# Attention stage with the transposes of the probabilities one unit behind the scores, a written-out order on four engines, and the gate row on ScalarE and GpSimd

## The chip, the cores and the metric

The kernel runs on one core of a Trainium2 chip. The time is device microseconds (us) of one run; three runs of the kernel before were timed, and their median counts. Five engines work side by side: TensorE (PE in the profile; PEld is its weight load), VectorE (DVE, `V` in the code), ScalarE (ACT, `S`), GpSimd (POOL, `G`) and SyncE (SP, `SY`), which here issues the loads and stores.

## The reference

One layer of a hybrid backbone, for one sequence of 512 latent tokens and 256 context tokens of width 2048: a common input projection, eight heads of a gated DeltaNet, eight heads of grouped-query attention (two key heads), gates on both, and one output projection. Everything is fp32. What bears on the change:

```python
mod = silu(c) @ w_ada + b_ada
shift, scale, gate = split(mod, 3)              # 2048 columns each
h = rms_norm(x, norm_w) * (1 + scale) + shift
qkv_g, z_g, gates, q_a, k_a, v_a, z_a = split_proj(h @ w_in)
...
s = einsum(q_blk, k_all) * HEAD_DIM ** -0.5     # 512 queries x 768 keys a head
p = softmax(s)
attn = einsum(p, v_all)
...
gdn_lat  = rms_norm(o_gdn, gdn_norm_w) * silu(z_g)
attn_lat = attn * silu(z_a)
y = concatenate([gdn_lat, attn_lat]) @ w_out
x = x + gate * y
return rms_norm(x, final_norm_w)
```

## The kernel before, in words

An fp32 product is made as three products of a high and a low half (`mm3`, lines 138 to 140): high x high, high x low, low x high. A weight piece of 128x512 is loaded by SP into `wraw`, ACT casts it to the high half `whi` (line 121), and POOL, or DVE where the caller says so, subtracts for the low half `wlo` (line 122). Each of the three has three buffers.

The program runs in stages. First come the modulation and the first projections, then the DeltaNet scans with further projections between them, up to about 924 us. Then comes the attention stage, which the change rewrites, to 1237.6 us, and then the output projection.

In the attention stage a head's 512 queries are taken as two units of 256 (`qp` 0 and 1, each with two blocks `qi` of 128). For a unit:

- `attn_scores`: PE makes the scores `s` (256 queries x 768 keys, one PSUM tile); DVE takes the maximum of each block (`mx`) and scales it, ACT makes exp and its sum (`pr`), DVE takes the reciprocal and scales `pr`.
- `attn_pt`: PE transposes `pr` in three groups of four blocks (tiles `pt`), ACT casts each to `pth`, DVE subtracts for `ptl`.
- `attn_values`: PE makes the output `o` from `pth`, `ptl` and the values, and DVE multiplies it into `M`, the input of the output projection.

`attn_norm` and `attn_qt` prepare the queries of the next head: `qtp` are transposes of the stored queries `qc` on PE; `qn` gets their norm (`hss`) and the rotary table, of which one product, `rt2`, is made on POOL; `qtp2` transposes back, and the halves are `qTh` and `qTl`.

PE would idle during the softmax, so the products of the gate path stand between: 16 tiles `zl`, each from 4 weight pieces, each piece 4 steps of 3 products. `fill(n)` puts n such steps at the place of the call; `FP`, `FS`, `FE`, `FV`, `FQ`, `FR` are the counts. After a tile, `z_steps` applies SiLU (ACT tanh, DVE `ze`) and multiplies into `M`. After every second head `gate_row` makes 512 columns of `gate`: 16 loads `graw` of `w_ada`, scaled and added up on DVE in `gacc` (line 1165), then summed over the partitions by a product with ones (`gater`) and stored.

After the stage, `M` is split into `mh` (ACT) and `ml` (DVE), and for each of four column blocks c the pieces of `w_out` (`wo`) are loaded and multiplied; `epilogue` applies gate, residual and final norm (`tt`, `yx`). For c below 3 the low half of an even piece k is made on POOL and of an odd one on DVE.

The order of PE's instructions is the order of the code throughout (`manual_schedule`); that of the other engines is set by the framework's scheduler. An engine runs its list in order.

## Time and profile before

| what | value |
|---|---|
| median of three runs | 1444.21 us (1441.69, 1444.21, 1445.38) |
| the profiled execution | 1441.82 us, span 1440.0 us, mean granted PE clock 0.976 |
| PE busy in the span | 1287.2 us (89%), 9406 instructions |
| PE weight load | 1027.4 us (71%) |
| DVE / ACT / POOL busy | 756.9 (53%) / 569.9 (40%) / 476.9 us (33%) |
| attention stage, 924.0 to 1237.6 us: PE / DVE / ACT / POOL busy | 288.77 / 189.98 / 123.63 / 100.58 of 313.60 us |

An engine's busy time is the sum of its recorded operations in the stretch. A group of instructions is shown by line, engine, operation and tiles (out<-in), with its count, busy time, mean and the idle time just before its members and what ended it. The granted clock is the share of full speed that the throttle gave PE.

### The profile page before, as it was taken

What the parts mean: (1) busy time and instruction counts of PE and PEld (TensorE: products, weight loads), DVE (VectorE), ACT (ScalarE), POOL (GpSimd) and SP (SyncE); (2) the same over time, 40 slices, a digit from 0 to 9 for tenths busy, and PEclk for the clock granted to TensorE, in tenths of its full rate; (3) what the DMA queues carried; (4) which work ended last, traced back from release to release, by engine and by line L of the source; (5) the groups of instructions that cost most, each with busy time, mean ns of one, the idle gap of its engine ahead of it and who ended that gap; (6) DMA issues with size and microseconds to landing.
All of it is one profiled execution on the core that took longest, in us unless ns stands there. A gap on an engine that the chain in (4) does not pass through costs nothing. (4 is left out here: it accounts for less than half of the span.)

```text
span 1440.0 us, 24845 instructions
## 1 busy us (share of the span) xinstructions
PE 1287.2 (89%) x9406; PEld 1027.4 (71%) x9406; DVE 756.9 (53%) x1680; ACT 569.9 (40%) x1441; POOL 476.9 (33%) x441
## 2 busy tenths in 40 slices
PE   3788888999998989898998988989898999998997
PEld 1455677888777777777777866777776777676785
DVE  3344694533756667665766243265747565433222
ACT  4111343343545454545444444334444433433221
POOL 1011212343343343434343444433333332233530
PEclk9999999999999999999999999999999999999999
DMA  9999522323222222131223432652525343464302
GB/s 307 264 287 283 152 67 62 66 71 81 55 68 48 61 57 60 44 74 50 61 56 69 119 105 70 189 170 69 163 71 153 81 126 95 155 228 137 93 28 107
DMA packets 263323, 161.95 MB, mean 112 GB/s; under 512 B 62946, under 2 KB 236091, under 8 KB 262179
## 3 DMA queue, kind: packets, MB, share of 16 engines
q1 hardware_dynamic: 263203, 160.36, 40.5%
q8 instruction: 74, 1.21, 0.3%
q14 instruction: 46, 0.38, 0.1%
HBM read 147.54 MB, written 12.77 MB: 111 GB/s over the span
## 5 line engine op out<-in xcount | busy, mean ns | idle before, releaser
L122 POOL TENSOR_TENSOR wlo_z<-wraw_z,whi_z 128x512 fp32r<-128x512 f32 x64 | 85.8, 1340 | 198.4 <-ACT whi_z L121 198.4
L156 PE MATMUL zl<-hhL,whi_z 128*128 128x512 f32 x256 | 108.6, 424 | 0.0
L156 PE MATMUL zl<-hlL,whi_z 128*128 128x512 f32 x256 | 103.4, 404 | 0.0
L214 POOL TENSOR_TENSOR sdh<-sth,egl 128x256 f32<-128x256 f32 x80 | 55.6, 695 | 142.6 <-DVE sth L756 68.3
L156 PE MATMUL zl<-hhL,wlo_z 128*128 128x512 f32 x256 | 102.5, 401 | 0.0
L735 ACT ACTIVATE oqh<-ksh,egsw 64x128 f32<-64x128 f32 x128 | 46.4, 362 | 118.9 <-DVE rh L730 118.1
L730 DVE SCALAR_TENSOR_TENSOR rh<-ksh,negeg,vtokh 64x128 f32<-64x128 f32 x176 | 61.3, 348 | 52.4 <-PE ksh L718 41.1
L139 PE MATMUL po<-wlo_wo,mh 128*128 128x512 f32 x192 | 77.0, 401 | 8.8 <-POOL wlo_wo L122 5.9
L138 PE MATMUL po<-whi_wo,mh 128*128 128x512 f32 x192 | 76.1, 399 | 1.7 <-ACT whi_wo L121 1.0
L140 PE MATMUL po<-whi_wo,ml 128*128 128x512 f32 x192 | 76.0, 396 | 0.0
L756 DVE TENSOR_TENSOR sth<-sdh,tsh 128x256 f32<-128x256 f32 x80 | 33.7, 421 | 76.8 <-PE tsh L750 56.4
L1165 DVE SCALAR_TENSOR_TENSOR gacc<-graw,scol,gacc 128x512 f32<-128x512 f32 x60 | 52.9, 882 | 22.4 <-DMA graw<-in_w_ada 21.8
L750 PE MATMUL tsh<-vsh,ktok 128*128 128x128 f32 x352 | 59.1, 291 | 5.7 <-ACT vnh L746 5.7
L122 POOL TENSOR_TENSOR wlo_wo<-wraw_wo,whi_wo 128x512 fp32r<-128x512 f32 x24 | 34.7, 1449 | 85.7 <-ACT whi_wo L121 85.7
L121 ACT CAST whi_z<-wraw_z 128x512 fp32r<-128x512 f32 x64 | 39.5, 618 | 53.8 <-PE zl L156 43.9
L750 PEld LDWEIGHTS tsh<-vsh,ktok 128*128 128x128 f32 x352 | 47.8, 195 | 17.6 <-ACT vnh L746 14.4
L122 POOL TENSOR_TENSOR wlo_qa<-wraw_qa,whi_qa 128x512 fp32r<-128x512 f32 x32 | 41.7, 1303 | 51.8 <-ACT whi_qa L121 42.8
L743 ACT ACTIVATE vsh<-tsh,cch 128x128 f32<-128x128 f32 x88 | 32.3, 367 | 64.5 <-PE tsh L739 61.6
L156 PEld LDWEIGHTS zl<-hhL,wlo_z 128*128 128x128 f32 x256 | 49.2, 192 | 12.0
L122 DVE TENSOR_TENSOR wlo_wo<-wraw_wo,whi_wo 128x512 fp32r<-128x512 f32 x24 | 19.9, 831 | 71.0 <-ACT whi_wo L121 68.5
L156 PEld LDWEIGHTS zl<-hhL,whi_z 128*128 128x128 f32 x256 | 49.4, 193 | 9.4 <-issue 0.8
L1109 PE MATMUL pt<-cmain,pr 128*128 128x128 f32 x192 | 33.4, 289 | 24.8 <-DVE pr L1098 18.3
(394 smaller groups left out, 3992.9 us busy)
## 6 DMA issues: line engine op xcount, KB each, us to landing
wada<-in_w_ada SPq DMA_DIRECT2D x128, 256.0 KB, 5.2
wraw_z<-in_w_in SPq DMA_DIRECT2D x64, 256.0 KB, 2.8
graw<-in_w_ada SPq DMA_DIRECT2D x64, 256.0 KB, 3.0
wraw_wo<-in_w_out SPq DMA_DIRECT2D x48, 256.0 KB, 2.9
wraw_qa<-in_w_in SPq DMA_DIRECT2D x32, 256.0 KB, 2.9
wraw_q<-in_w_in SPq DMA_DIRECT2D x28, 256.0 KB, 2.9
wraw_k<-in_w_in SPq DMA_DIRECT2D x28, 256.0 KB, 2.9
wraw_v<-in_w_in SPq DMA_DIRECT2D x28, 256.0 KB, 2.8
```

The costliest lines, as they stand in the source:

```text
L121: S.copy(hi, raw)
L122: (lo_eng or G).tensor_tensor(out=lo, in0=raw, in1=hi, op=ALU.subtract)
L138: T.matmul(out, lhsT=lh, rhs=rh, start=start, stop=False, skip_group_check=True)
L139: T.matmul(out, lhsT=lh, rhs=rl, start=False, stop=False, skip_group_check=True)
L140: T.matmul(out, lhsT=ll, rhs=rh, start=False, stop=stop, skip_group_check=True)
L156: T.matmul(pl, lhsT=lw, rhs=rt[0][:, k], start=st, stop=sp, skip_group_check=True)
L214: eng.tensor_tensor(out=out, in0=x, in1=y, op=ALU.mult)
L730: V.scalar_tensor_tensor(out=r[rows], in0=ks[rows, d], scalar=gsc["negeg"][rows, gcol:gcol + 1], in1=vtok[rows, p], op0=ALU.mult, op1=ALU.add)
L735: S.activation(oq[rows, v, p - 2], ks[rows, d], AF.Copy, scale=gsc["egsw"][rows, gcol:gcol + 1])
L750: T.matmul(ts[:, d], lhsT=ktok[:, p, half], rhs=vs, start=True, stop=True, skip_group_check=True)
L756: V.tensor_tensor(out=sn, in0=sd, in1=ts[:, 0:2], op=ALU.add)
L1165: V.scalar_tensor_tensor(out=acc, in0=raw, scalar=scol[:, k:k + 1], in1=acc, op0=ALU.mult, op1=ALU.add)
```

## The change

1. The loop over heads becomes a loop over 17 units `u`. In a turn PE makes the scores of unit u, and the transposes and values of unit u-1 (`before`). The counts of gate steps become `FS`, `FP`, `FQ`, `FR` = 3, 3, 1, 3; the first unit gets 8 more.
2. In the attention loop the order of ACT, DVE and POOL is also that of the code.
3. `attn_scores` makes both maxima and then both exponentials; reciprocal and scaling move to `attn_over`, which stands behind the first and second group of transposes. `attn_norm` is a generator in three parts, spread over the odd unit of a head; the queries are first copied to SBUF by ACT, and `qn` has one buffer.
4. `fillers` asks for a weight piece two pieces ahead. The end of a tile (`z_over`) comes in the second step of the next tile.
5. The gate row is made over the whole stage, about one addition per weight piece: ACT scales `graw` in place (into `gacc` for the first of a column block), and POOL adds it to `gacc`. `graw` has 3 buffers, `gacc` 2.
6. In the output projection, the low half is made on DVE for every k of c below 3.
7. The transposes of a group run over the query block outside and the key block inside.

The number of PE's products and of loads and stores is the same. The core of the diff, without the removed lines of functions that are printed above:

```diff
-FP, FS, FE, FV, FQ, FR = 2, 8, 2, 3, 2, 2
-GB, PB_, PR_ = 2, 3, 4
+FS, FP, FQ, FR = 3, 3, 1, 3
+GB = 3
...
     def attn_norm(h, qc):
         tp = transposes(qc, 0, 4, ttile([128, 4, 128], f"qtp{h}"))
-        qn = ap_.tile([128, 4, 128], F32, tag="qn", bufs=2, name=f"qn{h}")
+        qn = ap_.tile([128, 4, 128], F32, tag="qn", bufs=1, name=f"qn{h}")
...
+        S.copy(qn, tp)
+        for t in range(4):
+            S.activation(jk, qn[:, t], AF.Square, accum_out=ss[:, t:t + 1])
+        V.tensor_scalar(out=ss, in0=ss, scalar1=1.0 / 128.0, scalar2=EPS, op0=ALU.mult, op1=ALU.add)
+        power(ss, -0.5)
+        yield qn
+        mul(V, qn, qn, ss.unsqueeze(2).to_broadcast([128, 4, 128]))
+        t2 = ap_.tile([128, 4, 128], F32, tag="rt2", bufs=1, name=f"rt2{h}")
+        tb = A["tab"]
+        mul(G, t2.rearrange("p t (a s r) -> p (t a) s r", a=2, s=2), swapped(qn),
+            tb[:, 1].rearrange("p t (a s r) -> p (t a) s r", a=2, s=2))
+        yield qn
+        mul(V, qn, qn, tb[:, 0])
+        V.tensor_tensor(out=qn, in0=qn, in1=t2, op=ALU.add)
+        yield qn
...
         kv = h // 4
         sp = PSs.tile([128, 2 * NTOK], F32, tag="s", name=f"s{h}_{qp}")
+        sos = [sp[:, qi * NTOK:(qi + 1) * NTOK] for qi in range(2)]
+        mxs = [ap_.tile([128, 2], F32, tag="mx", bufs=4, name=f"mx{h}_{qp}_{qi}") for qi in range(2)]
+        for qi in range(2):
+            qsl = slice((qp * 2 + qi) * 128, (qp * 2 + qi + 1) * 128)
+            for c0, c1 in (((0, 512), (512, 768)) if qi == 0 else ((0, 256), (256, 768))):
+                mm3(sos[qi][:, c0:c1], qTh[:, qsl], qTl[:, qsl], kTh[:, kv, c0:c1], kTl[:, kv, c0:c1], True, True)
+        for qi in range(2):
+            V.tensor_reduce(out=mxs[qi][:, 0:1], in_=sos[qi], axis=AX.X, op=ALU.max)
+            V.tensor_scalar(out=mxs[qi][:, 0:1], in0=mxs[qi][:, 0:1], scalar1=-SC, scalar2=None, op0=ALU.mult)
         prs = []
         for qi in range(2):
...
+            pr = ap_.tile([128, NTOK], F32, tag="pr", bufs=4, name=f"pr{h}_{qp}_{qi}")
+            S.activation(pr, sos[qi], AF.Exp, bias=mxs[qi][:, 0:1], scale=SC, accum_out=mxs[qi][:, 1:2])
+            prs.append(pr)
+        return list(zip(prs, mxs))
+    def attn_over(pr, mx):
+        V.reciprocal(mx[:, 1:2], mx[:, 1:2])
+        V.tensor_scalar(out=pr, in0=pr, scalar1=mx[:, 1:2], scalar2=None, op0=ALU.mult)
+    def attn_pt(h, qp, prs, j2):
+        tp3 = ttile([128, 2, 256], f"pt{h}_{qp}_{j2}")
         for qi in range(2):
...
             for jj in range(2):
...
+                j = j2 * 2 + jj
+                T.transpose(out=tp3[:, jj, qi * 128:qi * 128 + 128],
+                            in_=prs[qi][0][:, j * 128:j * 128 + 128], identity=ident)
+        pth = ap_.tile([128, 2, 256], F32R, tag="pth", bufs=3, name=f"pth{h}_{qp}_{j2}")
+        ptl = ap_.tile([128, 2, 256], F32R, tag="ptl", bufs=3, name=f"ptl{h}_{qp}_{j2}")
+        split_from(tp3, pth, ptl)
+        return pth, ptl
     def attn_values(h, qp, pts):
         kv = h // 4
...
+    def z_over(i, pl):
         e = ap_.tile([128, SEQ], F32, tag="ze", bufs=2, name=f"ze{i}")
         S.activation(e, pl, AF.Tanh, scale=0.5)
         silu(V, e, pl, e)
...
+    def z_piece(n):
+        i, kq = divmod(n, 4)
+        col = (COL_ZG if i < 8 else COL_ZA - 1024) + i * 128
+        src = w_in[kq * 512:(kq + 1) * 512, col:col + 128].rearrange("(k p) c -> p k c", p=128)
+        return wpiece(src, f"z{i}_{kq}", 128)
     def fillers():
...
+        pieces = [z_piece(0), z_piece(1)]
+        over = None
+        yield
+        for n in range(64):
+            i, kq = divmod(n, 4)
+            if n + 2 < 64:
+                pieces.append(z_piece(n + 2))
+            for _ in range(1 + (n % 8 == 7)):
+                next(rows, None)
+            if kq == 2 and outs:
+                gate_out(*outs.pop(0))
+            hi, lo = pieces.pop(0)
+            if kq == 0:
+                pl = PP.tile([128, SEQ], F32, tag="pl", name=f"zl{i}")
+            for k4 in range(4):
+                k = kq * 4 + k4
+                for lw, rt, st, sp in ((hi[:, k4], hhL, k == 0, False), (hi[:, k4], hlL, False, False),
+                                       (lo[:, k4], hhL, False, k == KT - 1)):
+                    T.matmul(pl, lhsT=lw, rhs=rt[:, k], start=st, stop=sp, skip_group_check=True)
+                if over is not None and k == 1:
+                    z_over(*over)
+                yield
+            over = i, pl
+        z_over(*over)
+    def gate_out(c, acc, row):
         pr = PP.tile([128, 512], F32, tag="pl", name=f"gater{c}")
         T.matmul(pr[0:32], lhsT=ones[:, 0:32], rhs=acc, start=True, stop=True)
-        row = ap_.tile([128, 512], F32, tag="graw", bufs=GB, name=f"grow{c}")[0:1]
-        SY.dma_start(row, a["b_ada"][:, cb])
         V.tensor_tensor(out=row, in0=row, in1=pr[0:1], op=ALU.add)
         SY.dma_start(grd[:, c * 512:c * 512 + 512], row)
+    outs = []
+    def gate_rows():
+        def load(i):
+            c, k = divmod(i, KT)
+            raw = ap_.tile([128, 512], F32, tag="graw", bufs=GB, name=f"graw{i}")
+            SY.dma_start(raw, w_ada[k * 128:(k + 1) * 128, 2 * D + c * 512:2 * D + c * 512 + 512])
+            return raw
+        def bias(c):
+            row = ap_.tile([128, 512], F32, tag="ze", bufs=2, name=f"grow{c}")[0:1]
+            SY.dma_start(row, a["b_ada"][:, 2 * D + c * 512:2 * D + c * 512 + 512])
+            return row
+        raws = [load(i) for i in range(GB - 1)]
+        acc = last = None
+        yield
+        for i in range(4 * KT):
+            c, k = divmod(i, KT)
+            raw = raws.pop(0)
+            if k == 0:
+                last, acc = acc, ap_.tile([128, 512], F32, tag="gacc", bufs=2, name=f"gacc{c}")
+            S.activation(acc if k == 0 else raw, raw, AF.Copy, scale=scol[:, k:k + 1])
+            if k:
+                G.tensor_tensor(out=acc, in0=raw, in1=acc, op=ALU.add)
+            if i + GB - 1 < 4 * KT:
+                raws.append(load(i + GB - 1))
+            if k == 3 and c:
+                outs.append((c - 1, last, bias(c - 1)))
+            yield
+        outs.append((3, acc, bias(3)))
     qcs = {i: attn_q(i) for i in (1, 2)}
     for i in range(8):
         SY.dma_start(M[i], o_d[i])
+    rows = gate_rows()
+    next(rows)
     gen = fillers()
-    owed = [0]
+    es_m4 = ExitStack()
+    es_m4.enter_context(tc.manual_schedule(engines={mybir.EngineType.Activation, mybir.EngineType.DVE,
+                                                    mybir.EngineType.Pool}))
+    next(gen)
     def fill(n):
...
+        for _ in range(n):
+            next(gen, None)
     qt = A["qt"]
-    for h in range(NH):
+    before = None
+    for u in range(2 * NH + 1):
+        h, qp = divmod(u, 2)
         more = h + 1 < NH
-        p0_ = attn_scores(h, 0, *qt)
-        fill(FS)
+        prs = None
+        if h < NH:
+            prs = attn_scores(h, qp, *qt)
+            fill(FS + 8 * (before is None))
+        pts = []
+        for j2 in range(3):
+            if before is not None:
+                pts.append(attn_pt(*before, j2))
+            if prs is not None and j2 < 2:
+                attn_over(*prs[j2])
+            if qp == 1 and more and j2 in (0, 2):
+                qn = next(qns)
+            if before is not None:
+                fill(FP)
+        if before is not None:
+            attn_values(before[0], before[1], pts)
+            fill(FQ)
         if more:
...
+            if qp == 0:
+                qns = attn_norm(h + 1, qcs.pop(h + 1))
+                next(qns)
+                if h + 3 < NH:
+                    qcs[h + 3] = attn_q(h + 3)
+            else:
+                qt = attn_qt(h + 1, qn)
+            fill(FR)
+        before = h, qp, prs
     for _ in gen:
         pass
+    for _ in rows:
+        pass
+    for o_ in outs:
+        gate_out(*o_)
+    es_m4.close()
...
         if c < 3:
             ops = [PO.tile([128, 512], F32, tag="po", name=f"po{c}_{t}") for t in range(4)]
             for k in range(KT):
-                hi, lo = wpiece(w_out[k * 128:(k + 1) * 128, cs_], f"wo{c}_{k}", None, V if k % 2 else G)
+                hi, lo = wpiece(w_out[k * 128:(k + 1) * 128, cs_], f"wo{c}_{k}", None, V)
                 for t in range(4):
                     ts_ = slice(t * 128, t * 128 + 128)
                     mm3(ops[t], mh[k][:, ts_], ml[k][:, ts_], hi, lo, k == 0, k == KT - 1)
```

Two places in the order of the instructions. The first is the second half of head 1 on DVE, where the softmax of a unit and its `ptl` meet. Names end in head, unit and block (or group); line 211 is the SiLU of the gate path and 1141 (1150) its product into `M`. Before:

```order
L815 TENSOR_TENSOR ptl1_0_2_10282<-pt1_0_2_10276,pth1_0_2_10281 128x512
L1093 TENSOR_REDUCE mx1_1_0_10304<-s1_1_10291 128x1
L1094 TENSOR_SCALAR mx1_1_0_10304<-mx1_1_0_10304 128x1
L211 SCALAR_TENSOR_TENSOR ze2_10321<-ze2_10321,zl2_10173 128x512
L1141 SCALAR_TENSOR_TENSOR M2_9779<-ze2_10321,M2_9779 128x512
L1097 RECIPROCAL mx1_1_0_10304<-mx1_1_0_10304 128x1
L1093 TENSOR_REDUCE mx1_1_1_10311<-s1_1_10291 128x1
L1098 TENSOR_SCALAR pr1_1_0_10307<-pr1_1_0_10307,mx1_1_0_10304 128x768
L1094 TENSOR_SCALAR mx1_1_1_10311<-mx1_1_1_10311 128x1
L1097 RECIPROCAL mx1_1_1_10311<-mx1_1_1_10311 128x1
L1098 TENSOR_SCALAR pr1_1_1_10314<-pr1_1_1_10314,mx1_1_1_10311 128x768
L815 TENSOR_TENSOR qTl2_10370<-qtp22_10364,qTh2_10369 128x512
```

After, the row of the next unit, head 1 unit 1; lines 1113 and 1114 are reciprocal and scaling, 214 the products on `qn`, 1083 its sum:

```order
L815 TENSOR_TENSOR ptl1_0_0_10377<-pt1_0_0_10371,pth1_0_0_10376 128x512
L1113 RECIPROCAL mx1_1_0_10329<-mx1_1_0_10329 128x1
L1114 TENSOR_SCALAR pr1_1_0_10347<-pr1_1_0_10347,mx1_1_0_10329 128x768
L214 TENSOR_TENSOR qn2_10297<-qn2_10297,hss2_10298 128x512
L211 SCALAR_TENSOR_TENSOR ze2_10388<-ze2_10388,zl2_10183 128x512
L1150 SCALAR_TENSOR_TENSOR M2_9779<-ze2_10388,M2_9779 128x512
L815 TENSOR_TENSOR ptl1_0_1_10404<-pt1_0_1_10398,pth1_0_1_10403 128x512
L1113 RECIPROCAL mx1_1_1_10330<-mx1_1_1_10330 128x1
L1114 TENSOR_SCALAR pr1_1_1_10349<-pr1_1_1_10349,mx1_1_1_10330 128x768
L815 TENSOR_TENSOR ptl1_0_2_10434<-pt1_0_2_10428,pth1_0_2_10433 128x512
L214 TENSOR_TENSOR qn2_10297<-qn2_10297,tabq_8982 128x512
L1083 TENSOR_TENSOR qn2_10297<-qn2_10297,rt22_10383 128x512
```

The `ptl` of unit 0 now stand among the scalings of unit 1, and between them the norm of the next head's queries, then the SiLU and the product into `M`; before, `ptl` and scalings of the same unit followed each other. On POOL at the same place, before:

```order
L208 TENSOR_TENSOR hss2_10216<-hss2_10216,expo0_83 128x4
L214 TENSOR_TENSOR rt22_10225<-qn2_10215,tabq_8982 128x512
L122 TENSOR_TENSOR wlo_z3_1_10376<-wraw_z3_1_10373,whi_z3_1_10375 128x512
L122 TENSOR_TENSOR wlo_z3_2_10412<-wraw_z3_2_10409,whi_z3_2_10411 128x512
L122 TENSOR_TENSOR wlo_z3_3_10439<-wraw_z3_3_10436,whi_z3_3_10438 128x512
L122 TENSOR_TENSOR wlo_z4_0_10564<-wraw_z4_0_10561,whi_z4_0_10563 128x512
```

After; line 1225 is the addition of the gate row:

```order
L122 TENSOR_TENSOR wlo_z3_2_10360<-wraw_z3_2_10357,whi_z3_2_10359 128x512
L1225 TENSOR_TENSOR gacc0_9861<-graw13_10261,gacc0_9861 128x512
L214 TENSOR_TENSOR rt22_10383<-qn2_10297,tabq_8982 128x512
L122 TENSOR_TENSOR wlo_z3_3_10412<-wraw_z3_3_10409,whi_z3_3_10411 128x512
L1225 TENSOR_TENSOR gacc0_9861<-graw14_10320,gacc0_9861 128x512
L122 TENSOR_TENSOR wlo_z4_0_10445<-wraw_z4_0_10442,whi_z4_0_10444 128x512
L1225 TENSOR_TENSOR gacc0_9861<-graw15_10365,gacc0_9861 128x512
L122 TENSOR_TENSOR wlo_z4_1_10496<-wraw_z4_1_10493,whi_z4_1_10495 128x512
```

Between two low halves there now stands one addition, and the rotary product `rt22` of the next head's queries stands among them.

The second place is the handover to the output projection. On DVE, before:

```order
L1228 TENSOR_TENSOR ml13_12716<-M13_9790,mh13_12715 128x512
L1228 TENSOR_TENSOR ml14_12720<-M14_9791,mh14_12719 128x512
L1228 TENSOR_TENSOR ml15_12724<-M15_9792,mh15_12723 128x512
L122 TENSOR_TENSOR wlo_wo0_3_12806<-wraw_wo0_3_12803,whi_wo0_3_12805 128x512
L122 TENSOR_TENSOR wlo_wo0_5_12842<-wraw_wo0_5_12839,whi_wo0_5_12841 128x512
L122 TENSOR_TENSOR wlo_wo0_7_12878<-wraw_wo0_7_12875,whi_wo0_7_12877 128x512
```

After:

```order
L1300 TENSOR_TENSOR ml13_12787<-M13_9790,mh13_12786 128x512
L1300 TENSOR_TENSOR ml14_12791<-M14_9791,mh14_12790 128x512
L1300 TENSOR_TENSOR ml15_12795<-M15_9792,mh15_12794 128x512
L122 TENSOR_TENSOR wlo_wo0_3_12877<-wraw_wo0_3_12874,whi_wo0_3_12876 128x512
L122 TENSOR_TENSOR wlo_wo0_4_12895<-wraw_wo0_4_12892,whi_wo0_4_12894 128x512
L122 TENSOR_TENSOR wlo_wo0_5_12913<-wraw_wo0_5_12910,whi_wo0_5_12912 128x512
```

On POOL, before, where the last gate-path low halves are followed by the even pieces of `w_out`:

```order
L122 TENSOR_TENSOR wlo_z15_2_12535<-wraw_z15_2_12532,whi_z15_2_12534 128x512
L122 TENSOR_TENSOR wlo_z15_3_12562<-wraw_z15_3_12559,whi_z15_3_12561 128x512
L122 TENSOR_TENSOR wlo_wo0_0_12752<-wraw_wo0_0_12749,whi_wo0_0_12751 128x512
L122 TENSOR_TENSOR wlo_wo0_2_12788<-wraw_wo0_2_12785,whi_wo0_2_12787 128x512
L122 TENSOR_TENSOR wlo_wo0_4_12824<-wraw_wo0_4_12821,whi_wo0_4_12823 128x512
L122 TENSOR_TENSOR wlo_wo0_6_12860<-wraw_wo0_6_12857,whi_wo0_6_12859 128x512
```

The even pieces have moved from POOL's list to DVE's; there `wlo_wo0_4` and all that follow stand behind the sixteen `ml`.

72 lines of the change are left out of this document (removed).

## Prediction

> **What bounds the kernel now.** I looked first at the granted clock, then cut the span at the first score product (924.0 us) and the last gate-path product (1237.6 us). Columns of the windows view: length, then busy time and instructions of PE, weight load, DVE, ACT and POOL, granted clock, DMA share, GB/s.
>
> ```profile
> 924.00:1237.60 313.60, 288.77 (x1506) 235.72 (x1505) 189.98 (x310) 123.63 (x272) 100.58 (x77) 0.98 0.41 119
> 955.00:960.00 5.00, 4.54 (x17) 3.72 (x18) 3.70 (x6) 1.78 (x3) 0.73 (x1) 0.66 0.70 213
> 1015.00:1020.00 5.00, 3.95 (x15) 3.27 (x16) 3.08 (x6) 1.49 (x6) 2.88 (x3) 0.69 0.61 197
> 1110.00:1115.00 5.00, 3.77 (x15) 3.13 (x16) 3.63 (x5) 1.63 (x3) 1.73 (x2) 0.75 0.69 204
> 1115.00:1120.00 5.00, 5.00 (x24) 4.09 (x24) 3.06 (x5) 1.37 (x3) 1.34 (x2) 0.91 0.58 164
> 1190.00:1195.00 5.00, 5.00 (x20) 4.01 (x19) 3.53 (x6) 1.79 (x3) 1.73 (x1) 0.66 0.50 149
> ```
>
> PE is the bound of the attention stage, busy 288.77 of 313.60 us. What can be won there is its idle time, 24.8 us, and what the clock took: 5 x (1-0.66) = 1.7 and in the same way 1.55, 1.25 + 0.45 and 1.7, together 6.65 us. The list of who waited for whom, PE alone, says for what it stood still in the stage (us, times, longest):
>
> ```profile
> PE pt L1109 <- DVE pr L1098: 18.3, 12, 2.8
> PE pt L1109 <- DVE qn L804: 5.1, 4, 1.3
> PE pt L1109 <- DVE mx L1094: 1.4, 1, 1.4
> ```
>
> All of it is the transposes pt, waiting for the softmax that DVE finishes. The same list for the output projection, 1236 to 1441 us:
>
> ```profile
> PE po L139 <- POOL wlo_wo L122: 5.9, 6, 1.4
> PE po L139 <- DVE wlo_wo L122: 2.8, 2, 1.6
> PE po L138 <- ACT whi_wo L121: 1.0, 1, 1.0
> PE po L138 <- DVE tt L214: 0.6, 1, 0.6
> ```
>
> These are 10.3 us. So 24.8 + 6.65 + 10.3 = 41.8 us are open to this change; PE keeps every matmul that it has. Two rows of the timeline price a stall (idle time in brackets):
>
> ```profile
> 955.46 0.90 PE L1109 MATMUL pt<-cmain,pr 128*128 128x128 f32 x3 [2.15 <-DVE pr L1098]
> 1034.74 0.55 PE L1109 MATMUL pt<-cmain,pr 128*128 128x128 f32 x3 [1.84 <-DVE pr L1098]
> ```
>
> After the 2.15 us stall the clock fell to 0.66; after the 1.84 us one it did not. I take about 2.1 us as the edge and 1.7 us as its price.
>
> **What goes.** The pt of a unit (128x2 queries of one head) now come one unit later, so the softmax has a whole unit to be done, and all three waits on pr, qn and mx go as they stand. The 60 gate accumulations leave DVE. What is late next is the new order, fixed on ACT, DVE and POOL, so I walk it through one unit. The rows are groups of the stage (count | busy us, mean ns | idle):
>
> ```profile
> L1165 DVE SCALAR_TENSOR_TENSOR gacc<-graw,scol,gacc 128x512 f32<-128x512 f32 x60 | 52.9, 882 | 22.4 <-DMA graw<-in_w_ada 21.8
> L121 ACT CAST whi_z<-wraw_z 128x512 fp32r<-128x512 f32 x63 | 38.9, 618 | 51.6 <-PE zl L156 43.9 <-PE qal L156 4.4 <-issue 2.6
> L815 DVE TENSOR_TENSOR ptl<-pt,pth 128x512 fp32r<-128x512 f32 x48 | 32.9, 685 | 22.2 <-ACT pth L814 22.0
> L1093 DVE TENSOR_REDUCE mx<-s 128x1 f32<-128x768 f32 x32 | 30.3, 945 | 9.4 <-PE s L140 9.4
> L1098 DVE TENSOR_SCALAR pr<-pr,mx 128x768 f32<-128x768 f32 x32 | 28.9, 904 | 0.4
> L1096 ACT ACTIVATE pr<-s,mx 128x768 f32<-128x768 f32 x32 | 28.9, 902 | 50.1 <-DVE mx L1094 49.8
> L814 ACT CAST pth<-pt 128x512 fp32r<-128x512 f32 x48 | 28.1, 586 | 54.9 <-PE pt L1109 54.8
> L211 DVE SCALAR_TENSOR_TENSOR ze<-ze,zl 128x512 f32<-128x512 f32 x16 | 10.9, 681 | 13.1 <-ACT ze L1138 13.1
> L1141 DVE SCALAR_TENSOR_TENSOR M<-ze,M 128x512 f32<-128x512 f32 x15 | 10.3, 684 | 0.3
> L1096 ACT ACTIVATION_READ_ACCUMULATOR pr<-s,mx 128x1 f32 x32 | 6.2, 193 | 0.0
> L1097 DVE RECIPROCAL mx<-mx 128x1 f32<-128x1 f32 x32 | 5.1, 159 | 15.0 <-ACT pr L1096 15.0
> L214 DVE TENSOR_TENSOR qn<-qn,tabq 128x512 f32<-128x512 f32 x7 | 4.8, 693 | 5.7 <-POOL rt L214 5.7
> ```
>
> And PE's pace, from the chain (six gate products in 1.40, so 0.233 each) and the timeline (four transposes hold PE 0.35, and the product behind them 0.32 instead of 0.233, so 0.44 together):
>
> ```profile
> 1171.81 1.40 PE zl L156 x6
> 1130.88 0.60 PE L819 MATMUL qtp<-cmain,qc 128*128 128x128 f32 x4
> 1131.23 0.47 PE L156 MATMUL zl<-hhL,whi_z 128*128 128x512 f32 x1
> 1131.55 0.39 PE L156 MATMUL zl<-hlL,whi_z 128*128 128x512 f32 x1
> ```
>
> **PE's side.** From the end of a unit's scores: 9 gate products (2.10), then three times pt and 9 products (2.54), so the value product o starts at 9.72. Its columns are half as many, so I estimate half of 0.233 a piece: its last third, which needs the third ptl, starts at 9.72 + 12 x 0.117 = 11.12, the ptl itself at 11.24. o ends at 11.82, three products later, at 12.52, the transposes of the next head's queries (qtp) start; those are in every second unit, which I call odd.
>
> **The side of the others.** The first pth stands behind both exponentials, a whi cast and a gate scaling on ACT. mx 0.945, its scaling about 0.15 (as the reciprocal's 0.159), two exponentials with their sums 2 x 1.095, whi 0.618, the gate scaling (no row; 0.618 as the cast of the same tile, since both read and write 128x512 in SBUF; half or double of it moves only this slack), pth 0.586, ptl 0.685: 5.8. Then DVE, undisturbed, by its order: reciprocal 0.16, pr 0.60, [odd: qn by its norm 0.69], ze 0.68, M 0.68, ptl 0.69, reciprocal and pr 0.76, ptl 0.69. The third ptl is there at 10.05 in an even and 10.74 in an odd unit, ahead of 11.24. In odd units qn by the table and its sum follow, 2 x 0.69, done at 12.13, ahead of 12.52. Undisturbed, nothing stalls. But POOL disturbs (a source view, ns min/median/max; a neighbouring pair in the timeline; the group that prices a gate addition on POOL):
>
> ```profile
> L1098 DVE TENSOR_SCALAR pr<-pr,mx x32: 600/620/1645, 933.3 to 1224.3; 128x768 f32<-128x768 f32 x32
> 1346.88 1.29 POOL L1249 TENSOR_TENSOR yx<-yx,tt 128x512 f32<-128x512 f32 x1
> 1347.03 1.69 DVE L122 TENSOR_TENSOR wlo_wo<-wraw_wo,whi_wo 128x512 fp32r<-128x512 f32 x1 [3.62 <-ACT whi_wo L121]
> L1249 POOL TENSOR_TENSOR yx<-yx,tt 128x512 f32<-128x512 f32 x12 | 16.2, 1367 | 16.1 <-DVE tt L214 16.1
> ```
>
> DVE's subtraction began 0.15 us into POOL's addition and took 1.69 where the 0.69 of L214 would do: it stood until POOL was through. pr takes 0.60 alone and 0.904 on average, 0.30 more, with POOL busy 100.58 of 313.60, 32%. The gate's 60 additions put 60 x 1.367 = 82 us more on POOL, 183 in about 295, 62%. In proportion each DVE operation that touches only SBUF then waits 0.30 x 62/32 = 0.58. An even unit has three of them on the way (pr, M, pr), an odd one five (and the two on qn behind; the norm's falls while POOL itself waits for qn). Odd: 12.13 + 2.9 = 15.0, 2.5 behind 12.52; even: 10.05 + 1.74 = 11.8, 0.55 behind. Walking POOL's listed operations through one unit by these durations gave me 1.9 and 0. I take 2.2 for the 7 odd units and 0.2 for the 8 others: 15.4 + 1.6 = 17.0 us. Ends: 0 if all fits the slack; if each operation waits out a whole one of POOL (1.29), 5 x 1.29 + 12.13 - 12.52 = 6.1 and 3 x 1.29 + 10.05 - 11.24 = 2.7, together 64 and the clock on top. The odd wait falls in two parts, at o and at qtp, each under 1.84, so I charge no clock.
>
> The Trainium skill, page "SBUF — State Buffer", section "SBUF: two separate sides", speaks against the change here: DVE and GpSimd share a port pair "lock-allocated" by whole instructions, so the loser "fully blocks", for a DVE operation with two SBUF inputs or in a two-port mode. The 1.69 us row agrees. By that rule an operation waits on average half of POOL's 1.29 for 62% of the time, 0.40; the odd unit would lose 1.6, the units 11.2, and the time would be 1417.
>
> **Small terms.** First unit, 1.0: it has eleven steps of products and no pt, and its third whi waits behind both exponentials; PE stood longer there before. Output projection: all low halves go to DVE, so the 5.9 us on POOL go. Left is the handover: ACT's 15 casts and DVE's 15 subtractions (0.69 each, about 10.5 with the last gate operations) stand ahead of the fourth low half, which then is ready some 12 us after the last gate product; PE has o and three blocks of 12 x 0.233, 2.1 + 8.4 = 10.5. I charge 1.6 there and 1.0 for the rest; ends 0 and the present 10.3. Loads are the same in number; gate loads now wait on POOL's addition and stand ahead of weight loads on the SP queue, but each weight piece is asked for two pieces (some 8 us) ahead: 0.
>
> **Sum.** 41.8 go, 17.0 + 1.0 + 2.6 = 20.6 come, so 21.2 us less than the profiled execution's 1441.82 (span 1440.0), 1420.6. The median of the runs, 1444.21, lies 2.4 above it: 1423.
>
> **Rivals.**
> - POOL's collisions fall into the slack. For it: pr's median is 620. Against: POOL is back to back for 9 us of an odd unit. 41.8 - 3.6 = 38.2 less: 1406. Chance 0.15.
> - The two waits of an odd unit count together for the clock: 2.2 is over 2.15. 7 x 1.7 = 12 more: 1435. Chance 0.14. The Trainium skill, "TensorE: Matmul & The Clock Gate", section "Part 1: The HAM clock gate", asks for an idle window of about 3.4 us before the rate halves; by that rule this rival falls, but the trace shows the fall after 2.15 us.
> - Slower: the shared access of DVE and POOL becomes the bound. From a mean wait of 0.83 the part at o (3 x 0.83 - 0.5) also passes 2 us and takes the clock; with 1.0, odd units lose 4.6 + 1.7, even ones 1.8: 44 + 14 + 3.6 = 62, 20 more than now, 1464. For it: single waits of 1.0 (pr 1645). Against: the mean of 0.30. Chance 0.07.
> - The stage gains nothing because its order isn't kept or a load holds a queue: about 1438. Chance 0.04.
>
> **Numbers.** The forecast, 1411 to 1433, has 0.60. The range 1407 to 1438 takes in the clock's rival and stops short of the slower one and of the cleanest end. A change under 0.3% (4.3 us) can't be told from none: faster 0.86, same 0.07, slower 0.07.
>
> **What would show it.** Right: PE idle in the stage under 18 us and clock 1.00; no wait of pt for pr; the waits left are qtp for qn and o for ptl, on DVE, in odd units; pr's mean near 1.2 us; POOL busy near 180 us; no wait of po for POOL. Wrong: waits of zl for wlo or whi (POOL or ACT late with the pieces), pt still waiting, or the stage's clock at 0.98 or below.

## The result, and the profile after

The changed kernel took 1422.56 us (median of four runs, 1422.10 to 1424.98) against 1442.95 us for the kernel before (four runs, 1441.35 to 1445.38): ratio 0.9861, 95% interval 0.9841 to 0.9880. The forecast was 1423.0. Its profiled execution took 1422.10 us, span 1420.3, mean granted clock 0.982.

The span is cut here at the first score product and the first output product. Windows view, columns as in the prediction (length; busy time and instructions of PE, weight load, DVE, ACT, POOL; clock; DMA share; GB/s), the kernel before:

```profile
924.25:1237.62 313.37, 288.55 (x1505) 235.53 (x1504) 189.73 (x310) 123.63 (x272) 100.58 (x77) 0.98 0.42 119
1237.62:1440.00 202.38, 182.24 (x769) 143.44 (x767) 63.42 (x92) 60.50 (x114) 67.85 (x51) 0.98 0.39 129
```

and the changed kernel:

```profile
921.85:1225.29 303.44, 286.70 (x1505) 233.98 (x1504) 161.29 (x251) 163.37 (x347) 188.05 (x136) 0.99 0.43 122
1225.29:1420.30 195.01, 181.94 (x770) 144.92 (x768) 76.47 (x115) 58.73 (x110) 35.57 (x28) 0.97 0.40 134
```

The attention stage became 9.93 us shorter and the stretch behind it 7.37. The remaining 2.40 of the span's 19.7 lie ahead of the stage, in code that the change doesn't touch: over the kernels below, whose code there is the same, the stage begins anywhere from 917.7 to 927.3 us. That is why the experiments are read by the length of the stage first.

What PE waited for from 921 to 1225.3 us, and from there to the end (total, times, longest):

```profile
PE qtp L819 <- DVE qn L1083: 10.3, 7, 3.0
PE o L139 <- DVE ptl L815: 5.6, 16, 0.6
PE gater L1196 <- DVE ze L211: 0.5, 1, 0.5
PE zl L1186 <- POOL wlo_z L122: 0.2, 1, 0.2
```

```profile
PE po L139 <- DVE wlo_wo L122: 1.8, 3, 1.3
PE po L138 <- DVE M L214: 1.1, 1, 1.1
PE po L138 <- ACT whi_wo L121: 0.5, 1, 0.5
```

No transpose of the probabilities waits any more; 24.8 us of such waits became 16.6 us of others, at the two places named beforehand. One odd unit on PE shows them (timeline, idle time in brackets):

```profile
987.80 0.27 PE L138 MATMUL o<-pth,vah 128*128 128x256 f32 x1
988.28 0.39 PE L139 MATMUL o<-ptl,vah 128*128 128x256 f32 x1 [0.21 <-DVE ptl L815]
988.51 0.28 PE L140 MATMUL o<-pth,val 128*128 128x256 f32 x1
...
988.98 0.28 PE L138 MATMUL o<-pth,vah 128*128 128x256 f32 x1
989.84 0.38 PE L139 MATMUL o<-ptl,vah 128*128 128x256 f32 x1 [0.57 <-DVE ptl L815]
990.06 0.28 PE L140 MATMUL o<-pth,val 128*128 128x256 f32 x1
...
992.69 0.63 PE L819 MATMUL qtp<-cmain,qn 128*128 128x128 f32 x4 [1.30 <-DVE qn L1083]
```

and on DVE and POOL at the same time:

```profile
983.97 1.11 DVE L1114 TENSOR_SCALAR pr<-pr,mx 128x768 f32<-128x768 f32 x1
...
986.31 1.31 DVE L1150 SCALAR_TENSOR_TENSOR M<-ze,M 128x512 f32<-128x512 f32 x1
987.55 0.68 DVE L815 TENSOR_TENSOR ptl<-pt,pth 128x512 fp32r<-128x512 f32 x1
...
988.34 0.85 DVE L1114 TENSOR_SCALAR pr<-pr,mx 128x768 f32<-128x768 f32 x1
989.10 0.68 DVE L815 TENSOR_TENSOR ptl<-pt,pth 128x512 fp32r<-128x512 f32 x1
989.70 1.16 DVE L214 TENSOR_TENSOR qn<-qn,tabq 128x512 f32<-128x512 f32 x1
990.89 1.65 DVE L1083 TENSOR_TENSOR qn<-qn,rt 128x512 f32<-128x512 f32 x1
```

```profile
983.37 1.30 POOL L1225 TENSOR_TENSOR gacc<-graw,gacc 128x512 f32<-128x512 f32 x1
985.76 1.32 POOL L214 TENSOR_TENSOR rt<-qn,tabq 128x512 f32<-128x512 f32 x1 [1.10 <-DVE qn L214]
987.04 1.72 POOL L122 TENSOR_TENSOR wlo_z<-wraw_z,whi_z 128x512 fp32r<-128x512 f32 x1
988.73 1.59 POOL L1225 TENSOR_TENSOR gacc<-graw,gacc 128x512 f32<-128x512 f32 x1
990.27 1.72 POOL L122 TENSOR_TENSOR wlo_z<-wraw_z,whi_z 128x512 fp32r<-128x512 f32 x1
```

PE waits 0.21 + 0.57 + 1.30 = 2.1 us in this unit, as in four more of the seven odd ones; in four of the even units it waits 0.2. On DVE the first scaling of pr takes 1.11, the product into `M` 1.31, the sum of `qn` 1.65, while the `ptl`, which read PSUM, keep 0.68. DVE stands idle nowhere from 983.17 until the sum of `qn` ends; it is the operations themselves that are long. Each of the five long ones begins while an operation of POOL runs, and ends 0.4 to 0.55 us behind that operation's end: 985.08 behind 984.67, 987.62 behind 987.08, 989.19 behind 988.76, 990.86 behind 990.32, 992.54 behind 991.99.

### The profile page after: what moved, and what is told of

Read it like the earlier page. It is cut to its first block, busy times and chain, and to the rows that moved or that the text cites. A ratio compares the mean times of both kernels' runs of the same rounds, so it can differ in the third digit from the quotient of the medians.

```text
span 1420.3 us, 24982 instructions
## 1 busy us (share of the span) xinstructions
PE 1282.4 (90%) x9406; PEld 1024.6 (72%) x9406; DVE 741.2 (52%) x1642; ACT 608.5 (43%) x1511; POOL 533.0 (38%) x477
## 5 line engine op out<-in xcount | busy, mean ns | idle before, releaser
L122 POOL TENSOR_TENSOR wlo_z<-wraw_z,whi_z 128x512 fp32r<-128x512 f32 x64 | 92.5, 1448 | 80.4 <-ACT whi_z L121 72.1
L1225 POOL TENSOR_TENSOR gacc<-graw,gacc 128x512 f32<-128x512 f32 x60 | 85.1, 1418 | 0.5
L122 DVE TENSOR_TENSOR wlo_wo<-wraw_wo,whi_wo 128x512 fp32r<-128x512 f32 x48 | 37.8, 794 | 59.5 <-ACT whi_wo L121 59.3
L1321 POOL TENSOR_TENSOR yx<-yx,tt 128x512 f32<-128x512 f32 x12 | 17.2, 1446 | 127.8 <-DVE tt L214 127.8
L815 DVE TENSOR_TENSOR ptl<-pt,pth 128x512 fp32r<-128x512 f32 x48 | 32.8, 683 | 53.5 <-ACT pth L814 53.5
L1103 DVE TENSOR_REDUCE mx<-s 128x1 f32<-128x768 f32 x32 | 30.5, 953 | 53.9 <-PE s L140 53.9
```

The source lines that it names most:

```text
L122: (lo_eng or G).tensor_tensor(out=lo, in0=raw, in1=hi, op=ALU.subtract)
L815: V.tensor_tensor(out=lo, in0=ps_ap, in1=hi, op=ALU.subtract)
L1225: G.tensor_tensor(out=acc, in0=raw, in1=acc, op=ALU.add)
```

## The experiments

All ratios are to the kernel before, which was timed anew beside each group of runs (medians 1441.14 to 1442.95 us), with 95% intervals; "stage" is the length from the first score product to the first output product in the profiled execution.

| run | median, us | ratio | stage, us |
|---|---|---|---|
| changed kernel | 1422.56 | 0.9861 (0.9841 to 0.9880) | 303.4 |
| low_half_dve | 1437.13 | 0.9957 (0.9933 to 0.9982) | 309.7 |
| low_half_split | 1429.74 | 0.9905 (0.9868 to 0.9942) | 303.6 |
| no_gate_adds | 1413.41 | 0.9792 (0.9756 to 0.9827) | 289.8 |
| query_early | 1417.28 | 0.9824 (0.9792 to 0.9857) | 292.6 |
| m_late | 1424.73 | 0.9879 (0.9841 to 0.9917) | 305.0 |
| same_unit | 1428.82 | 0.9896 (0.9857 to 0.9936) | 303.6 |
| gate_on_dve | 1417.74 | 0.9823 (0.9784 to 0.9863) | 296.3 |
| free_order | 1443.32 | 1.0001 (0.9973 to 1.0029) | 322.2 |
| m_late_out | 1411.52 | 0.9779 (0.9754 to 0.9804) | 288.7 |
| same_unit_out | 1420.61 | 0.9850 (0.9824 to 0.9876) | 298.3 |
| late_gate_dve | 1407.95 | 0.9751 (0.9724 to 0.9779) | 285.2 |
| late_query | 1403.54 | 0.9716 (0.9688 to 0.9745) | 282.0 |

The two runs whose stage is a repetition show how far a stage length can be trusted: low_half_split has the changed kernel's (303.6 and 303.4), low_half_dve that of the kernel before (309.7 and 313.4, a clock dip and 2.2 us of waits fewer). So a difference of 4 us between two stages proves little.

### The low halves of w_out

low_half_dve, on the kernel before:

```diff
-                hi, lo = wpiece(w_out[k * 128:(k + 1) * 128, cs_], f"wo{c}_{k}", None, V if k % 2 else G)
+                hi, lo = wpiece(w_out[k * 128:(k + 1) * 128, cs_], f"wo{c}_{k}", None, V)
```

> The kernel before with one edit: all low halves of w_out on DVE (part 6 alone). The waits of po fell from 10.3 to 3.4 us with the whole change, and the stretch from the first po to the end became 7.4 us shorter. Theory: that is part 6 by itself, so about 1436 us against 1443, the 5.9 us of po waiting for POOL gone, the attention stage as before (24.8 us of pt waits). Rival: the low halves are only in time because the new attention stage leaves DVE and ACT in another state at the handover; then DVE, with 16 ml ahead of it, becomes the wait, and the time stays within 0.3% of 1443.

low_half_split, on the changed kernel:

```diff
-                hi, lo = wpiece(w_out[k * 128:(k + 1) * 128, cs_], f"wo{c}_{k}", None, V)
+                hi, lo = wpiece(w_out[k * 128:(k + 1) * 128, cs_], f"wo{c}_{k}", None, V if k % 2 else G)
```

> The changed kernel with part 6 undone (even low halves back on POOL). Theory: it gives back 6 to 7.5 us, 1429 to 1430 against 1422.6, with waits of po for POOL near 6 us, and the stage as in the changed kernel. Rival: POOL is freer at the end of the new stage (the gate additions are over 30 us before it), so the low halves come in time there: 1422 to 1424.

The stretch behind the stage is 198.0 us in the first (before: 202.4), 200.4 in the second (changed: 195.0). In low_half_split PE waits there for POOL again:

```profile
PE po L139 <- POOL wlo_wo L122: 4.8, 6, 1.4
```

So by this stretch the edit is worth 4.4 us by itself and 5.4 in the changed kernel, less than the 6 to 7.5 expected (the medians of low_half_split and the changed kernel lie 7.2 us apart, but their intervals overlap); the other 2 to 3 of the 7.4 came with the new stage. The rival of low_half_split falls by the 4.8 us of waits above. That of low_half_dve falls by the waits, since none of `po` for POOL is left there; by the time alone it is not excluded, as the interval of the ratio reaches 0.9982.

### Is it POOL that makes DVE's operations long?

no_gate_adds, on the changed kernel:

```diff
             S.activation(acc if k == 0 else raw, raw, AF.Copy, scale=scol[:, k:k + 1])
-            if k:
-                G.tensor_tensor(out=acc, in0=raw, in1=acc, op=ALU.add)
```

> The changed kernel without the 60 additions of the gate row on POOL (the loads and the scalings on ACT stay; the gate row is left out of the result). Theory, collisions of DVE and POOL: with POOL busy some 100 instead of 188 us of the stage, pr falls from 0.98 to about 0.75 us, qn plus rt from 1.66 to about 0.7, the qtp waits (10.3 us) to under 2 outside the first odd unit, the o waits (5.6) to under 2, and with the restart costs and the one clock dip the time is 1404 to 1410. Rival, the order of DVE's list alone makes the waits: they stay at 15.9 us, and the time within 0.3% of 1422.6.

DVE's list is the same in both kernels. In the changed one:

```profile
L1114 DVE TENSOR_SCALAR pr<-pr,mx 128x768 f32<-128x768 f32 x32 | 31.3, 977 | 1.1
L1083 DVE TENSOR_TENSOR qn<-qn,rt 128x512 f32<-128x512 f32 x7 | 11.6, 1664 | 0.2
```

without the additions:

```profile
L1114 DVE TENSOR_SCALAR pr<-pr,mx 128x768 f32<-128x768 f32 x32 | 24.3, 761 | 1.1
L1083 DVE TENSOR_TENSOR qn<-qn,rt 128x512 f32<-128x512 f32 x7 | 4.8, 690 | 0.2
...
PE o L139 <- DVE ptl L815: 3.3, 6, 0.6
PE qtp L819 <- DVE qn L1083: 2.5, 6, 0.8
```

The same operations in the same list are 0.2 and 1.0 us shorter with 60 operations of another engine gone; the waits fall from 15.9 to 5.8 us, the one clock dip goes, and the stage is 13.7 us shorter. The rival falls. The waits that remain, 3.3 and 2.5 us, are more than the 2 us that I had expected of each at most. (The time, 1413, is above the expected 1404 to 1410 mainly because the profiled execution's stage began 4.5 us later than the changed kernel's.) `M` stays long (1.31 in the mean), since a product or a low half of POOL runs beside it in either case.

gate_on_dve puts the same work on the other engine:

```diff
-            S.activation(acc if k == 0 else raw, raw, AF.Copy, scale=scol[:, k:k + 1])
-            if k:
-                G.tensor_tensor(out=acc, in0=raw, in1=acc, op=ALU.add)
+            if k == 0:
+                V.tensor_scalar(out=acc, in0=raw, scalar1=scol[:, k:k + 1], scalar2=None, op0=ALU.mult)
+            else:
+                V.scalar_tensor_tensor(out=acc, in0=raw, scalar=scol[:, k:k + 1], in1=acc, op0=ALU.mult, op1=ALU.add)
```

> The changed kernel with the gate row back on DVE, at the same places in the code (60 operations of 0.88 us in the kernel before, four a unit; ACT's scalings and POOL's additions go). Theory, collisions: pr, M and the queries' sum lose their waits on POOL as without the additions (qn plus rt from 1.66 to 0.7), but two or three of the gate's own operations stand ahead of the third ptl and three or four ahead of the queries' sum, 0.7 to 0.9 each; the waits at o and qtp stay about as they are or grow by up to 1 us a unit: stage 300 to 320. Rival: the idle 3.4 us of DVE in each unit takes them in and only the freed POOL counts: stage 290 to 294, as without the additions.

DVE is busy 206.4 us of the stage instead of 161.3, and the stage is 7.1 us shorter. `qtp` waits 0.3 us in all, because `qn` plus `rt` is back at 0.69; what is left is at `o`:

```profile
L1226 DVE SCALAR_TENSOR_TENSOR gacc<-graw,scol,gacc 128x512 f32<-128x512 f32 x60 | 57.2, 954 | 0.3
...
PE o L139 <- DVE ptl L815: 12.5, 11, 1.6
```

The theory as I had put it (waits as they are or longer, 300 us and more) is wrong here: DVE's idle time swallowed most of the additions, though not all, as the rival had it. What the theory had right is the wait at `o`, which grew from 5.6 to 12.5 us, and `pr` still takes 0.92, so that not all collisions are gone. By the length of the stage, having moved the gate row to ACT and POOL costs the changed kernel 7 us against spreading it over DVE at the same places; the medians lie 4.8 us apart and their intervals overlap.

### Where the two chains stand

query_early takes the queries' chain out from between the `ptl`:

```diff
             prs = attn_scores(h, qp, *qt)
+            if qp == 1 and more:
+                next(qns)
             fill(FS + 8 * (before is None))
+            if qp == 1 and more:
+                qn = next(qns)
...
-            if qp == 1 and more and j2 in (0, 2):
-                qn = next(qns)
```

> The changed kernel with the norm and the rotary products of the next head's queries moved on DVE and POOL from between and behind the ptl to right behind the maxima, where DVE stands idle 3.4 us in each unit. Theory: qtp waits for qn no more (11.5 us with the restarts, and 1.7 of clock), the second ptl wait of odd units goes too (4 us idle, about 5 with restarts); 1404 to 1408. Rival: the three operations and the POOL product collide there as they did behind, end after the first pth is there, and push the three ptl back: the wait at o grows by as much as qtp loses, 1418 to 1425.

`qtp` waits no more, and the waits at `o` fall from 5.6 to 3.5 us. In the first odd unit the chain waits for a POOL that is still behind, and stops the `ptl`: one wait of 2.62 us with a clock dip. The stage is 10.9 us shorter; without that wait and its dip (2.6 and 1.7 us) it would have been some 15 us shorter, about what the theory had. The time of the profiled execution would still be above the expected 1404 to 1408, because its stage began 4.9 us later than the changed kernel's.

m_late moves the other work out of the way:

```diff
-                if over is not None and k == 1:
+                if over is not None and k == 7:
                     z_over(*over)
                 yield
-            over = i, pl
+            if kq == 3:
+                over = i, pl
```

> The changed kernel with the end of a gate tile (ze and its product into M) six steps later, so that on DVE both stand behind the third ptl instead of ahead of the second. Theory: the chain ahead of the ptl loses 0.68 + 1.2 to 1.3 us, which is more than the waits left at o (0.21 and 0.57 us idle), and the queries' sum ends 2 us earlier, more than the 1.3 us that qtp waits; both waits go in every unit but the first odd one, where about 1 us stays and takes no clock. The attention stage falls from 303.4 to 283 to 286 us, the time to about 1404. Rival: the waits come from the collisions wherever the operations stand; ze and M then collide beside the queries' sum or the next maxima, qtp still waits about 1 us in odd units and s or pt in the next: stage 295 to 303.

`o` waits no more, but a new wait ate it: `gater`, eight steps into a tile, needs the PSUM buffer that the late `ze` still reads.

```profile
PE gater L1197 <- DVE ze L211: 11.8, 4, 5.6
```

m_late_out moves `gater` one piece on:

```diff
-            if kq == 2 and outs:
+            if kq == 3 and outs:
```

> The run m_late with the column sum of the gate row (gater) one weight piece later, since it took the PSUM buffer that the later ze still held. Theory: the 12.5 us that gater cost PE there go and nothing takes their place, so the stage is 292 to 294 us, with qtp waiting 0.93 us in each odd unit and o not at all. Rival: the next gate tile needs the buffer that gater frees late and waits instead: stage 298 to 305.

The stage is 288.7, better than expected, and what is left is the wait of `qtp`, in the odd units. I had expected m_late to end that wait as well, and its rival was right that it stays at about 1 us; `qn` plus `rt` still takes 1.66, since the collision goes where the operation goes.

late_gate_dve is gate_on_dve with the edits of m_late_out; late_query is m_late_out with the norm, `rt2` and the product with the table right behind the maxima (from the second odd unit on) and the sum behind the third `ptl`:

```diff
         mul(V, qn, qn, tb[:, 0])
+        yield qn
         V.tensor_tensor(out=qn, in0=qn, in1=t2, op=ALU.add)
...
             prs = attn_scores(h, qp, *qt)
+            if qp == 1 and more and u > 1:
+                next(qns)
             fill(FS + 8 * (before is None))
+            if qp == 1 and more and u > 1:
+                next(qns)
...
-            if qp == 1 and more and j2 in (0, 2):
+            if qp == 1 and more and j2 == 2 or u == 1 and j2 < 2:
                 qn = next(qns)
```

> The run gate_on_dve (gate row on DVE, stage 296.3 us, all of its waits at o) with ze and M behind the third ptl and gater one piece later. Theory: o's 15.8 us go, because 1.9 us of DVE work leave the chain ahead of the ptl and POOL, with only the low halves, rarely stands in the way: stage 280 to 284 us, the shortest of all. Rival: ze, M and four gate operations of 0.9 us then push the maxima of the next unit, and pt or o waits there: 288 to 296.

> The run m_late_out (gate row on POOL) with the norm, the POOL product and the product with the table of the next head's queries right behind the maxima from the second odd unit on, and only their sum behind the third ptl. Theory: the six qtp waits (6.6 us with restarts) go: stage 285 to 288 us. Rival: the collisions move with the operations; the first ptl comes late and pt or o waits about 0.5 us in odd units, 290 to 293.

late_gate_dve reaches 285.2, just over its range: `qtp` waits 2.4 us in all. late_query is the shortest, below its 285 to 288:

```profile
925.96:1207.96 282.00, 280.38 (x1505) 232.59 (x1504) 158.27 (x251) 163.87 (x347) 188.56 (x136) 1.00 0.47 131
PE o L139 <- DVE ptl L815: 1.0, 1, 1.0
PE s L140 <- DVE qTl L815: 0.4, 1, 0.4
L1115 DVE TENSOR_SCALAR pr<-pr,mx 128x768 f32<-128x768 f32 x32 | 32.8, 1026 | 1.1
```

POOL is as busy as in the changed kernel and `pr` even longer (1.03 against 0.98 us): the collisions are all still there, and cost 1.4 us of PE's time, because each operation now has slack behind it. At 1403.54 us this kernel beats both, by 2.8% the one before (ratio 0.9716).

### Lag or order?

same_unit undoes part 1: transposes and values come in the unit's own turn, behind 8 steps, with the order by hand and ze and M late.

```diff
-FS, FP, FQ, FR = 3, 3, 1, 3
+FS, FP, FQ, FR = 8, 2, 1, 1
...
-    for u in range(2 * NH + 1):
+    for u in range(2 * NH):
...
             prs = attn_scores(h, qp, *qt)
-            fill(FS + 8 * (before is None))
+            for p_ in prs:
+                attn_over(*p_)
+            fill(FS)
+            before = h, qp, prs
...
-            if prs is not None and j2 < 2:
-                attn_over(*prs[j2])
```

> Part 1 undone, with the orders written out by hand: the transposes and values of a unit come in the unit's own turn, behind 8 steps of gate products (counts FS, FP, FQ, FR = 8, 2, 1, 1, the same 16 a unit), the scalings of pr right behind the exponentials, ze and M behind them as in the run before. From scores to both pr DVE and ACT need 2.2 (maxima) + 1.1 (second exponential) + 0.15 + 0.62 to 1.1, so 4.1 to 4.6 us; 8 steps give PE 5.6. Theory that the lag is what took the waits of pt away: with all the softmax in one turn pt waits again, over 10 us in the stage, 310 us or more. Rival, the order by hand is what took them away and the lag isn't needed: pt waits under 4 us, the stage 284 to 296.

Its stage, 303.6, lies between the theory and the rival. `pt` waits 4.4 us in all, and only for DVE to free its PSUM buffer. It has `gater`'s wait as m_late has (4.5 + 1.3 us); same_unit_out moves that on as well.

> The run same_unit (no lag) with gater one weight piece later, as in m_late_out. Theory now: the order by hand took the waits of pt away, and the lag is worth only what the last small waits (pt for a free PSUM buffer 4.4 us idle, qtp) cost; gater's 6.6 us go, the stage is 296 to 298 us, 3 to 6 us longer than m_late_out. Rival: without the lag the pieces and gate tiles meet the softmax in another place and new waits of pt come up: over 302 us.

```profile
PE pt L1122 <- DVE ptl L815: 5.7, 13, 0.5
```

No `pt` waits for `pr`, `qn` or `mx`: the lag isn't needed to take those waits away. That the order by hand took them, as the rival has it, does not follow, since free_order below has none of them either, with the lag and without that order. By the stage the lag is worth 298.3 - 288.7 = 9.6 us, more than the 3 to 6 I gave it. (The two kernels differ in the counts too, so this is the price of the pair.)

free_order undoes part 2:

```diff
-    es_m4.enter_context(tc.manual_schedule(engines={mybir.EngineType.Activation, mybir.EngineType.DVE,
-                                                    mybir.EngineType.Pool}))
```

> The changed kernel with part 2 undone: ACT, DVE and POOL ordered by the framework again. On POOL up to three additions of the gate row then stand between two low halves, twelve of the first column block ahead of the piece z2_0. Theory: low halves come late and zl waits for wlo (no such wait is in the changed kernel beyond 0.2 us), the clock falls behind the longer ones; stage 315 to 340. Rival: the additions wait for their loads and scalings anyway and the lag hides the rest: stage within 5 us of 303.

Stage 322.2, as the theory said, but by another way: `zl` waits 0.5 us for a low half in all. PE waits at `pt`, for DVE to free its buffer:

```profile
PE pt L1122 <- DVE ptl L815: 28.2, 6, 7.4
```

One of the six, on DVE and POOL; PE's `pt` started at 1044.16 after 7.16 us:

```profile
1034.20 0.69 DVE L214 TENSOR_TENSOR qn<-qn,hss 128x512 f32<-128x512 f32 x1 [1.33 <-POOL hss L208]
1038.57 1.74 DVE L214 TENSOR_TENSOR qn<-qn,tabq 128x512 f32<-128x512 f32 x1 [2.57 <-POOL rt L214]
1040.23 1.61 DVE L1114 TENSOR_SCALAR pr<-pr,mx 128x768 f32<-128x768 f32 x1
...
1043.43 0.68 DVE L815 TENSOR_TENSOR ptl<-pt,pth 128x512 fp32r<-128x512 f32 x1
...
1029.18 4.02 POOL L1225 TENSOR_TENSOR gacc<-graw,gacc 128x512 f32<-128x512 f32 x3
1033.15 1.01 POOL L208 TENSOR_TENSOR hss<-hss,expo 128x4 f32<-128x4 f32 x1
```

The framework put the queries' chain ahead of the first `ptl`, and that chain waits for POOL twice, the first time behind three additions. All else being as in the change, the time is that of the kernel before (ratio 1.0001): without the order by hand, the other parts win nothing in sum. The stretch behind the stage keeps its gain (195.7 us against 202.4 before), and the stage is 8.8 us longer than before. No `pt` waits for `pr`, `qn` or `mx` here, so these waits are gone with the lag but without the order, as they are in same_unit_out with the order but without the lag. Parts 3, 4 and 7 were not undone as a whole in any run.

## Why the prediction was right

By its own steps:

- **What goes.** Right: all waits of `pt` on pr, qn and mx are gone. The reason given, that the pt come one unit later, holds only in part. With the lag and without the order by hand (free_order) they are gone, but same_unit_out has none of them either, without the lag. What else took them there stays open.
- **POOL's share and the wait of a DVE operation.** POOL was forecast busy 183 us and 62%; it was 188.05 of 303.44, 62%. An operation's wait was put at 0.58: in the unit shown, pr, M and pr lost 0.49, 0.63 and 0.23 (1.11, 1.31 and 0.85 against 0.62, 0.68 and 0.62), `qn` by the table 0.47 and its sum 0.96, 0.56 in the mean. The mean of pr, 0.98, is below the 1.2 I named: over all 32 scalings the loss is 0.98 - 0.60 = 0.38. So the proportion to POOL's 62% did not hold; the chain shown loses more because POOL works beside it nearly throughout (rows above, without a break from 985.76 on), and that its mean came near 0.58 is luck.
- **Odd and even units.** 2.2 us in an odd unit, 2.1 measured in the one shown; 0.2 in an even one, 0 to 0.24 measured. Together 17.0 and 1.0 for the first unit were forecast; 16.6 was measured, 3.8 of it in the first odd unit and 0.2 in the first one. The rule of the Trainium skill, page "SBUF — State Buffer", section "SBUF: two separate sides", that the loser is blocked until the other's instruction is through, agrees with the rows: DVE's operations ended only behind the one of POOL that they had met, and no_gate_adds shows that POOL was the reason. The estimate made from that page, 1.6 for an odd unit, was low, since it took POOL as busy 62% of the time beside this chain too.
- **Output projection.** 2.6 of the 10.3 us were to remain; 3.4 did, of it 1.4 near the handover, where I had 1.6. But most of the 1.4 is not the wait for a low half that I had named: 1.1 us is PE waiting for DVE's product of the last `o` into `M` (in the other units ACT copies `o` into `M`), and 0.3 for a low half.
- **The clock: the term that was mis-sized.** I had all of the 6.65 us gained. The first odd unit waited 2.97 us at `qtp`, and the clock fell:

```profile
950.00:955.00 5.00, 2.03 (x9) 1.53 (x8) 3.58 (x3) 0.52 (x2) 3.04 (x2) 0.80 0.42 120
955.00:960.00 5.00, 5.00 (x23) 4.12 (x22) 0.84 (x2) 2.30 (x4) 3.48 (x3) 0.85 0.42 114
```

That is 1.0 + 0.75 = 1.75 us. The cause is one operation that I had left out of the walk, the first split of `M`, which stands in DVE's list between `qn` by the table and the sum, and collides too. In the code it stands behind the loop (line 1300), where the framework sets the order again, and the framework placed it there:

```profile
950.15 1.76 DVE L1300 TENSOR_TENSOR ml<-M,mh 128x512 fp32r<-128x512 f32 x1
951.84 1.75 DVE L1083 TENSOR_TENSOR qn<-qn,rt 128x512 f32<-128x512 f32 x1
```

In m_late_out the same split comes behind the sum, the first odd unit waits 0.90 us at `qtp` as the others do, and the clock stays at 1.00 there.

- **A cost that was missing: what a short stall takes beyond its idle time.** In the rows of `o` above, the stall of 0.21 us idle moved the next start from 0.12 to 0.48 us away (988.28 - 987.80) and the one behind it from 0.12 to 0.23: 0.47 in all; that of 0.57 cost 0.74 + 0.10 = 0.84. The product before a stall drains without the next one running beside it, and the first behind it starts slow: 0.26 us a stall by these two, which I take as an estimate for the others. The kernel before had 17 stalls in the stage, the changed one 25.

The stage was to give 24.8 + 6.65 - 18.0 = 13.45 us and gave 9.93. The idle time came out 1.4 better than forecast (16.6 against 18.0), the clock 1.75 worse, and about 8 more stalls at 0.26 are 2.1; 1 us is not accounted for. In the profiled pair 2.40 us ahead of the stage, which owe nothing to the change, made up for most of that: by its own stretches the change won 17.3 of the 21.2 us. That the median came within 0.5 us of the forecast is therefore partly luck.

- **Rivals.** The clean one (1406) fell to the collisions. The clock's (2.2 us as one stall) did not come about: behind the later odd units the clock stayed at 1.00, with 1.5 us of products between their two longer waits (989.84 to 992.69 - 1.30). The mechanism of the slower one was at work, but with a mean wait of 0.56 us in the unit shown it stayed below the 0.83 from which it would have decided.

## What to carry to other kernels

Before an engine is given more work "because it is idle", look whether its operations hold up those of a neighbour that stands on the critical chain: here 85 us of additions on POOL, off the path themselves, made the stage 13.7 us longer than it is without them. Such collisions need not be removed; it was enough to order DVE's list by what PE needs next and give everything else slack, which is what the last 19 us came from. And an experiment that undoes each part alone is worth it: the part in the change's name, the lag, was not needed to remove the waits of `pt`, though without it the stage is longer.

## What the runs showed that I had not expected

- POOL pays too: beside DVE's SBUF operations its own grow from 1.30 to 1.72 us (rows above), so both engines lose in one collision.
- The clock has no sharp edge. In m_late `gater` waits twice for 2.04 us, and the clock fell behind the first of these stalls and not behind the second (timeline, then windows behind each: length, PE busy, clock, DMA share, GB/s):

```profile
1004.14 1.33 PE L1197 MATMUL gater<-gacc,cmain 128*32 128x512 f32 x2 [2.04 <-DVE ze L211]
1080.14 1.05 PE L1197 MATMUL gater<-gacc,cmain 128*32 128x512 f32 x2 [2.04 <-DVE ze L211]
1006.00:1009.00 3.00, 3.00 (x13) 0.64 0.68 188
1082.00:1085.00 3.00, 3.00 (x23) 1.00 0.71 182
```

So my edge of 2.1 us was good for a forecast and no more. The Trainium skill, page "TensorE: Matmul & The Clock Gate", section "Part 1: The HAM clock gate (the "warmup" mystery)", calls the window free-running, and with that these rows agree, though none shows the window itself: the same idle time decides differently at different moments. Its length of about 3.4 us of idle time is not what these traces show: the clock fell after 2.04, 2.15 and 2.97 us.
